# Second inverse norm of the output projection behind four output additions, and five sums of squares moved from GpSimd to VectorE, in a one-layer Fourier / RG-LRU / PEER kernel

## The chip, the cores and the metric

The kernel runs on one core of a Trainium2 chip. The time is device microseconds (us) of one launch; the lower the better. The engines are named as in the profile: PE is the matrix engine (PEld its weight loads), DVE is VectorE, ACT is ScalarE, POOL is GpSimd, SP is the engine that issues most transfers.

## The reference

One layer works on 512 latent tokens of width 1024, with 256 context tokens that feed the recurrences. What matters here is the middle, where two head groups are normalised, joined, projected and added, and the second norm is taken:

```python
rx = ((lat_dirs[0] + lat_dirs[1]) * gelu(gx)).astype(x.dtype)
mx = concatenate([rmsnorm(fourier_mix(fx), fourier_out_g[l]),
                  rmsnorm(rx, lru_out_g[l])], axis=-1) @ w_out[l]
x = x + g1_x * mx
h2x = modulate(rmsnorm(x, norm2_g[l]), sh2_x, sc2_x)
x = x + g2_x * peer_ffn(h2x, ...)
```

`rmsnorm` multiplies by the inverse root of the mean square over the width. `peer_ffn` makes queries from `h2x`, takes the best keys, and sums the experts that they choose out of a table of 16384; it is by far the longest part of the run.

## The kernel before

Everything is kept transposed: width on the 128 partitions (eight blocks `x2[0]` to `x2[7]` of 128x512), tokens along the row. Float32 products are made of three matmuls of a high and a low part (`mm3`), so each operand is split: ACT writes the high part (`act(hi, ...)`), DVE or POOL the low part, a subtraction.

The output projection is the loop `for k in range(8)` near the end of the first phase. `out_mm(k)` multiplies half of the normalised heads by one block of output weights into two PSUM banks: k = 0 to 3 use the Fourier heads `Ys`, k = 4 to 7 the recurrent heads `mr`. There are five such banks (tag "ps"), so `out_mm(0)`, `out_mm(1)` and the first half of `out_mm(2)` fill them, and the next half must wait until an `out_add` has read one.

- `out_add(k, ..., rF)` for k < 4 multiplies a bank by the gate and by the Fourier inverse norm `rF` on DVE (L650, reads PSUM and one SBUF tile) and adds the product to `x2` on POOL (L651, reads two SBUF tiles). For k of 4 and more one DVE instruction adds the bank to `x2` (L647).
- `rsqrt` (L148 to L154) makes an inverse norm: one ACT instruction, then L151 (DVE, reads PSUM) and L152, L153, L154 (DVE, each with two SBUF tiles), each needing the one before. It is called for `rF` and for `r`, the inverse norm of the recurrent branch.
- `rec_norm(k)` makes one of the four tiles of `mr`: `rx * r` on POOL (L630, two SBUF tiles), high part on ACT, low part on DVE (L579). `out_mm(4)` needs all four.
- `out_weights(k)` splits a block of output weights: high part `whi` on ACT, low part `wlo` on DVE (L123).
- `x2_sums(k)` squares two blocks of `x2` on ACT and adds the squares of blocks 0 to 5 up in `sq2` (L669); blocks 6 and 7 and `sq2` are then summed over the partitions by matmuls with ones (L666, L667, L664), which gives `rstd2`. Blocks 0 and 1 are squared after `out_add(5)`, 2 and 3 after `out_add(6)`, 4 and 5 after `out_add(7)`.

Behind the loop stand the last columns of the modulation (`mod_mm(20)` to `mod_mm(23)`, L232, and `half_turned(23)`, L240), then the second norm (L742, L744 and ACT), which makes `h2h` and `h2l`, on which all of `peer_ffn` rests. The splits of the first query weights (`wpq`, on DVE) and of the first expert weights `u` (on POOL, L123 as well) are already under way here.

PE, ACT and DVE run the first phase in the order in which the code is written: `in_order` ties each instruction to the one before on its engine. POOL's and SP's order is the scheduler's.

Of the kernel before, what the change touches and what calls it, by code (L numbers as in the profile page):

```python
# [9 lines left out]
F32 = mybir.dt.float32  # L10
# [5 lines left out]
ALU = mybir.AluOpType  # L16
# [35 lines left out]
def build(tc, xT, ctxT, c2t, vecs, wm, wu, wf, wg, wgate, wo, wq, keys, u, v, urow, vrow,  # L52
# [3 lines left out]
    V, S, G, PE = nc.vector, nc.scalar, nc.gpsimd, nc.tensor  # L56
# [8 lines left out]
    def act(o, i, f, bias=None, scale=None, **kw):  # L65
        if bias is not None:
            kw["bias"] = bias
        if scale is not None:
            kw["scale"] = scale
        return S.activation(o, i, f, **kw)  # L70
# [32 lines left out]
    def tact(*a, **kw):  # L103
        ins = act(*a, **kw).ins
        after(ins, last[0], "activation table order")
        last[0] = ins

    def pst(tag="ps", n=512, dt=F32):
        return psum.tile([P, n], dt, tag=tag, name="ps_" + tag, bufs={"ps": 5, "pm": 1, "pa": 2}[tag])

    def load(ap, st="", cuts=1):
        t = raws.tile([P, 2048], F32, tag="raw" + st, name="raw")
        n = 2048 // cuts
        for c in range(cuts):
            nc.sync.dma_start(t[:, c * n:(c + 1) * n], ap[:, c * n:(c + 1) * n])
        return t
# [9 lines left out]
    def split_w(raw, h, lo_eng=None, st=""):  # L126
        return split((wspl.tile([P, 1024], F32R, tag="whi" + st, name="whi"),
                      wspl.tile([P, 1024], F32R, tag="wlo" + st, name="wlo")),
                     raw[:, h * 1024:(h + 1) * 1024], lo_eng)
# [18 lines left out]
    def rsqrt(r, m, ss, n):  # L148

        tact(r, ss, AF.Abs_reciprocal_sqrt, bias=epst, scale=1.0 / n)  # L150
        V.tensor_scalar(m, ss, 1.0 / n, EPS, op0=ALU.mult, op1=ALU.add)  # L151
        V.scalar_tensor_tensor(m, m, -0.5, r, op0=ALU.mult, op1=ALU.mult)  # L152
        V.tensor_tensor(m, m, r, op=ALU.mult)  # L153
        V.scalar_tensor_tensor(r, m, 1.5, r, op0=ALU.add, op1=ALU.mult)  # L154
# [10 lines left out]
    def bt(dt=F32, n=L):  # L165
        return bp.tile([P, n], dt, tag="b", name="b")
# [18 lines left out]
    def mod_load_b(n):  # L185

        rawm[n] = ahead.get(n) or [bt()[:, :512] for j in range(4)]
        for j, t in enumerate(rawm[n]):
            nc.sync.dma_start(t, wm[n // 8, n % 8, :, j * 512:(j + 1) * 512])
# [29 lines left out]
    def mod_mm(n):  # L219
        t = rawm.pop(n)  # L220
        if n < 8 or n >= 16:


            m, first, final = -1 - n // 4, n % 4 == 0, n % 4 == 3
            ds = [2 * (n % 4) + j // 2 for j in range(4)]
        else:
            m, first, final = n // 8, n % 8 == 0, n % 8 == 7
            ds = [n % 8] * 4
        if first:
            modp[m] = pst("pm")  # L230
        for j in range(4):
            PE.matmul(modp[m][32 * j:32 * j + 32], cc32[:, ds[j]], t[j], start=first, stop=final)  # L232

    def half_turned(n):

        sb = bt(F32, 512)
        act(sb, modp[-1 - n // 4], AF.Copy)
        pT = pst("pa", 32)
        for b in range(4):
            PE.matmul(pT[:, 4 * b:4 * b + 4], sb[:, b * P:(b + 1) * P], vec[:, V_SEL2:V_SEL2 + 4], start=True, stop=True)  # L240
        return pT[:, :16].rearrange("p (b j z) -> p z j b", b=4, j=2)

    def half_biased(pv, o, outs):
        for k, mm in enumerate(outs):
            V.tensor_tensor(mm[:, o:o + 8].rearrange("p (j b) -> p j b", j=2), pv[:, k],
                            vec[:, V_BMOD + o:V_BMOD + o + 8].rearrange("p (j b) -> p j b", j=2), op=ALU.add)
# [220 lines left out]
    def mod_cols(w, st=""):  # L467
        mod_load(8 + w, st)
        if w:
            mod_mm(7 + w)  # L470
        if w == 8:
            mod_out(1)
# [67 lines left out]
    def out_weights(k):  # L540
        wp = split_w(rawo[k // 2], k % 2, V, ("", "U")[k // 2 % 2])
        if k % 2 and k < 4:
            rawo.append(load(wo[2 + k // 2]))
        return wp
# [83 lines left out]
    def rec_norm(k):  # L628
        rx = hsum[k][:, C:]
        G.tensor_tensor(rx, rx, r, op=ALU.mult)  # L630
        mr.append(scaled_split(rx, vec[:, V_LG + k:V_LG + k + 1]))

    def out_mm(k, wp, ms):
        pss = []
        for e in range(2):
            ps = pst("ps")
            for c in range(NB):
                o = (e * 4 + c) * P
                mm3(ps, cut(wp, slice(o, o + P)), ms[c], c == 0, c == NB - 1)
            pss.append(ps)  # L640
        return pss

    def out_add(k, pss, r=None):
        for e in range(2):
            d = 2 * (k % 4) + e
            if r is None:
                V.scalar_tensor_tensor(x2[d], pss[e], mods[:, 16 + d:17 + d], x2[d], op0=ALU.mult, op1=ALU.add)  # L647
            else:
                t = bt(F32, 512)
                V.scalar_tensor_tensor(t, pss[e], mods[:, 16 + d:17 + d], r, op0=ALU.mult, op1=ALU.mult)  # L650
                G.tensor_tensor(x2[d], x2[d], t, op=ALU.add)  # L651

    sq2 = bt(F32, 512)
    ss2 = []

    def x2_sums(k):
        if k == 3:
            ss2.append(pst("pa"))
        for e in range(2):
            d = 2 * k + e  # L660
            sq = bt(F32, 512) if d else sq2
            act(sq, x2[d], AF.Square)
            if d == ND - 1:
                PE.matmul(ss2[0], ones, sq, start=False, stop=True)  # L664
            elif d == ND - 2:
                PE.matmul(ss2[0], ones, sq2, start=True, stop=False)  # L666
                PE.matmul(ss2[0], ones, sq, start=False, stop=False)  # L667
            elif d:
                G.tensor_tensor(sq2, sq2, sq, op=ALU.add)  # L669

    psk = {}
    for k in range(8):
        psk[k] = out_mm(k, wpo[k], Ys if k < 4 else mr)
        if k == 1:
            ssf, ssr = pst("pa"), pst("pa")
            PE.matmul(ssf, ones, Y0, start=True, stop=True)
            PE.matmul(ssr, ones, sqr, start=True, stop=True)
            rF = bt(F32, 512)
            rsqrt(rF, bt(F32, 512), ssf, 512)
            r = bt(F32, 512)  # L680
            rsqrt(r, bt(F32, 512), ssr, 512)
            out_add(0, psk[0], rF)
        if k:
            out_add(k, psk[k], rF if k < 4 else None)
        if k > 4:
            x2_sums(k - 5)
        if k + 4 < 8:
            wpo[k + 4] = out_weights(k + 4)
        if 0 < k < 3:
            rec_norm(2 * k - 2)  # L690
            rec_norm(2 * k - 1)
        if k < 3:
            mod_cols(9 + k, "U")
        if k == 3:
            mod_mm(19)
        if k == 5:
            half_biased(half_turned(19), 32, (mods,))
        if k in (3, 4):
            mod_load_b(14 + 2 * k)
            mod_load_b(15 + 2 * k)  # L700
        if k == 5:
            raw0 = load(wq[0])
        if k == 6:
            wpq = [split_w(raw0, p, V) for p in range(2)]
    x2_sums(3)
    rsqrt(rstd2, bt(F32, 512), ss2[0], 1024)
    for n in range(20, 24):
# [257 lines left out]
    for ch in range(NCH):  # L965
# [14 lines left out]
        for q in range(TC // 4):  # L980
            ps = pst()
            for t in range(4):
                o = ps[:, t * P:(t + 1) * P]
                k, r = 2 * q + t // 2, t % 2
# [226 lines left out]
    for g in order:  # L1211
# [9 lines left out]
        sq = phase_v(g, cur, nxt)  # L1221
# [101 lines left out]
```

## Time and profile before

| | us |
|---|---|
| median of 3 runs | 1462.14 |
| lowest and highest of them | 1456.86, 1463.33 |
| the profiled execution | 1457.23 |
| its span, first to last instruction | 1455.5 |
| PE busy | 1386.5 |
| DVE busy | 1234.6 |
| POOL busy | 685.3 |

The output projection and the second norm lie between 185 and 250 us of the span. The times in the rows below are microseconds from the start of the span.

### The profile page before, as it was taken

The page shows a single profiled execution, that of the slowest core. Times are in us where ns is not written, and L with a number is a line of the kernel's source. Part 1 is how long each engine was busy: PE and PEld are TensorE (multiplying, and loading weights), DVE is VectorE, ACT ScalarE, POOL GpSimd, SP SyncE. Part 2 cuts the span into 40 slices and gives each one's busy share as a digit, 9 for nine tenths or more (in the row PEclk, how much of TensorE's full clock was granted, in tenths as well). Part 3 has the DMA queues.
Part 4 walks back from the last instruction along what each step waited for, and adds up shares of the span by engine and source line. Part 5 has one row for each costly group of instructions (what it writes and reads, how often), then busy time and mean ns, then how long its engine had stood idle before and what let it go on. Part 6 is the DMA issues. An engine that isn't in the chain of part 4 may idle for free. (4 is left out here: it accounts for less than half of the span.)

```text
span 1455.5 us, 22655 instructions
## 1 busy us (share of the span) xinstructions
PE 1386.5 (95%) x8577; PEld 1282.2 (88%) x8577; DVE 1234.6 (85%) x2185; ACT 614.5 (42%) x882; POOL 685.3 (47%) x462
## 2 busy tenths in 40 slices
PE   6998898999989999999999999999999999899995
PEld 2776766888969999999999999999999999899995
DVE  5677876599987999598998889999898989999973
ACT  4567634433434656434343432434333343243351
POOL 0044163666520000465666757675675766644412
PEclk9999999999999999999999999999999999999997
DMA  9334465331326999999999998999999999999901
GB/s 348 153 116 150 169 230 183 136 114 63 112 91 202 307 302 319 365 379 355 399 373 416 337 394 328 413 376 379 406 377 375 390 364 416 409 415 416 394 33 57
DMA packets 133645, 420.61 MB, mean 289 GB/s; under 512 B 10784, under 2 KB 60192, under 8 KB 110496
## 3 DMA queue, kind: packets, MB, share of 16 engines
q1 hardware_dynamic: 86976, 251.04, 46.5%
q0 software_dynamic: 46560, 168.14, 29.9%
q8 instruction: 67, 1.10, 0.3%
q14 instruction: 42, 0.34, 0.1%
HBM read 385.41 MB, written 33.69 MB: 288 GB/s over the span
## 5 line engine op out<-in xcount | busy, mean ns | idle before, releaser
L70 ACT ACTIVATE whi<-raw 128x1024 fp32r<-128x1024 f32 x296 | 312.7, 1060 | 589.1 <-PE ps_pa L133 291.6
L123 DVE TENSOR_TENSOR wlo<-raw,whi 128x1024 fp32r<-128x1024 f32 x264 | 327.0, 1241 | 41.4 <-ACT whi L70 39.3
L132 PE MATMUL ps_pa<-h2h,whi 128*128 128x352 f32 x1024 | 334.9, 327 | 3.2 <-ACT act L70 3.2
L134 PE MATMUL ps_pa<-h2h,wlo 128*128 128x352 f32 x1024 | 333.0, 325 | 0.2 <-DVE wlo L123 0.2
L133 PE MATMUL ps_pa<-h2l,whi 128*128 128x352 f32 x1024 | 332.6, 325 | 0.0
L1106 POOL DMA_INDIRECT row<-vrow,eidx x128 | 193.4, 1511 | 131.9 <-DVE oacc L1127 95.1
L1106 POOL DMA_INDIRECT row<-urow,eidx x128 | 198.3, 1549 | 110.7 <-DVE row L1113 56.8
L133 PE MATMUL ps_ps<-wl,whi 128*128 128x352 f32 x640 | 207.3, 324 | 0.0
L134 PE MATMUL ps_ps<-wh,wlo 128*128 128x352 f32 x640 | 206.7, 323 | 0.1
L132 PE MATMUL ps_ps<-wh,whi 128*128 128x352 f32 x640 | 206.1, 322 | 0.0
L132 PEld LDWEIGHTS ps_pa<-h2h,whi 128*128 128x128 f32 x1024 | 192.9, 188 | 5.3 <-ACT act L70 4.0
L134 PEld LDWEIGHTS ps_pa<-h2h,wlo 128*128 128x128 f32 x1024 | 192.7, 188 | 1.4 <-DVE wlo L123 0.5
L133 PEld LDWEIGHTS ps_pa<-h2l,whi 128*128 128x128 f32 x1024 | 192.7, 188 | 1.1
L1113 DVE SCALAR_TENSOR_TENSOR row<-row,hrow 128x1024 f32<-128x1024 f32 x128 | 153.6, 1218 | 32.6 <-DMA row<-urow,eidx 32.4
L1127 DVE SCALAR_TENSOR_TENSOR oacc<-row,gw,oacc 128x1024 f32<-128x1024 f32 x127 | 162.4, 1279 | 8.6 <-DMA row<-vrow,eidx 8.1
L134 PEld LDWEIGHTS ps_ps<-wh,wlo 128*128 128x128 f32 x640 | 120.2, 188 | 0.4 <-DVE wlo L123 0.4
L133 PEld LDWEIGHTS ps_ps<-wl,whi 128*128 128x128 f32 x640 | 120.2, 188 | 0.0
L132 PEld LDWEIGHTS ps_ps<-wh,whi 128*128 128x128 f32 x640 | 120.1, 188 | 0.0
L123 POOL TENSOR_TENSOR wlo<-raw,whi 128x1024 fp32r<-128x1024 f32 x32 | 77.5, 2422 | 84.1 <-ACT whi L70 57.8
L133 PE MATMUL ps_pa<-wl,whi 128*128 128x352 f32 x256 | 82.9, 324 | 0.0
L134 PE MATMUL ps_pa<-wh,wlo 128*128 128x352 f32 x256 | 82.6, 323 | 0.0
L132 PE MATMUL ps_pa<-wh,whi 128*128 128x352 f32 x256 | 82.3, 322 | 0.0
(303 smaller groups left out, 2606.4 us busy)
## 6 DMA issues: line engine op xcount, KB each, us to landing
raw<-u SPq DMA_DIRECT2D x64, 1024.0 KB
raw<-v SPq DMA_DIRECT2D x64, 1024.0 KB
Gd<-stg SPq DMA_DIRECT2D x22, 1024.0 KB
gt<-Gd SPq DMA_DIRECT2D x16, 1408.0 KB
raw<-wm SPq DMA_DIRECT2D x16, 1024.0 KB
b<-wm SPq DMA_DIRECT2D x32, 256.0 KB
raw<-wq SPq DMA_DIRECT2D x8, 1024.0 KB
Ad<-act SPq DMA_DIRECT2D x10, 704.0 KB
```

The costliest lines, as they stand in the source:

```text
L70: return S.activation(o, i, f, **kw)
L123: lo_ins[0] = (lo_eng or V).tensor_tensor(dst[1], src, dst[0].bitcast(F32), op=ALU.subtract).ins
L132: PE.matmul(ps, a[0], b[0], start=start, stop=False)
L133: PE.matmul(ps, a[0], b[1], start=False, stop=False)
L134: PE.matmul(ps, a[1], b[0], start=False, stop=stop)
L1106: G.indirect_dma_start(out=t, out_offset=None, in_=tab, in_offset=bass.IndirectOffsetOnAxis(ap=e[:, s:s + 1], axis=0))
L1113: ins = V.scalar_tensor_tensor(t, t, 1.0, hr, op0=ALU.mult, op1=ALU.mult, accum_out=dt[:, s:s + 1])
L1127: ins = V.scalar_tensor_tensor(o, t, g[:, s:s + 1], o, op0=ALU.mult, op1=ALU.add)
```

## The change

Two edits. The call that makes `r` now stands behind `out_add(0)` and `out_add(1)`. And the additions into `sq2` (five: blocks 1 to 5) go to VectorE instead of GpSimd.

```diff
             elif d:
-                G.tensor_tensor(sq2, sq2, sq, op=ALU.add)
+                V.tensor_tensor(sq2, sq2, sq, op=ALU.add)
...
             rF = bt(F32, 512)
             rsqrt(rF, bt(F32, 512), ssf, 512)
-            r = bt(F32, 512)
-            rsqrt(r, bt(F32, 512), ssr, 512)
             out_add(0, psk[0], rF)
         if k:
             out_add(k, psk[k], rF if k < 4 else None)
+        if k == 1:
+            r = bt(F32, 512)
+            rsqrt(r, bt(F32, 512), ssr, 512)
```

On DVE, at `k == 1` of the loop, the difference reads as follows (`-` is before, `+` is after; `ps_ps` are the banks of `out_mm`, `ps_pa` the sum of squares, `b` SBUF tiles of the first phase).

```order
 L154 SCALAR_TENSOR_TENSOR b<-b 128x512
+L650 SCALAR_TENSOR_TENSOR b<-ps_ps,mods,b 128x512 x4
 L151 TENSOR_SCALAR b<-ps_pa 128x512
 L152 SCALAR_TENSOR_TENSOR b<-b 128x512
 L153 TENSOR_TENSOR b<-b 128x512
 L154 SCALAR_TENSOR_TENSOR b<-b 128x512
-L650 SCALAR_TENSOR_TENSOR b<-ps_ps,mods,b 128x512 x4
 L123 TENSOR_TENSOR wlo<-raw,whi 128x1024
 L579 SCALAR_TENSOR_TENSOR b<-b,vec 128x512 x2
```

The four products of the first two output additions have moved ahead of the four instructions that make `r`; what follows stands as it did.

On POOL, at the same place, the scheduler answers with another order (`x_83` to `x_90` are `x2[0]` to `x2[7]`).

```order
 L588 TENSOR_TENSOR b<-b 128x512 x3
-L630 TENSOR_TENSOR b<-b 128x512 x2
 L651 TENSOR_TENSOR x_83<-x_83,b 128x512
-L630 TENSOR_TENSOR b<-b 128x512
 L651 TENSOR_TENSOR x_84<-x_84,b 128x512
-L630 TENSOR_TENSOR b<-b 128x512
 L651 TENSOR_TENSOR x_85<-x_85,b 128x512
 L651 TENSOR_TENSOR x_86<-x_86,b 128x512
+L630 TENSOR_TENSOR b<-b 128x512 x4
 L651 TENSOR_TENSOR x_87<-x_87,b 128x512
```

Before, two of the four products with `r` stood ahead of the first addition to `x2` and the other two between the next ones; now all four stand behind four such additions.

On DVE again, at the end of the loop, around the splits of the first query weights.

```order
 L647 SCALAR_TENSOR_TENSOR x_87<-ps_ps,mods,x_87 128x512
 L647 SCALAR_TENSOR_TENSOR x_88<-ps_ps,mods,x_88 128x512
+L669 TENSOR_TENSOR b<-b 128x512 x2
 L123 TENSOR_TENSOR wlo<-raw,whi 128x1024 x2
 L647 SCALAR_TENSOR_TENSOR x_89<-ps_ps,mods,x_89 128x512
 L647 SCALAR_TENSOR_TENSOR x_90<-ps_ps,mods,x_90 128x512
+L669 TENSOR_TENSOR b<-b 128x512 x2
 L151 TENSOR_SCALAR b<-ps_pa 128x512
```

Four of the five moved additions stand here, two ahead of the weight splits and two behind the last output addition; the fifth stands earlier, behind `x_86`. On SP one load of expert weights (`raw<-u`) moves ahead of the 16 loads `b<-wm` of the last modulation columns; PE's and ACT's orders are unchanged, and so is every order behind the second norm.

## Rows read from the trace of the kernel before

**Rows 1.** The page: busy time, share of the span and instructions of each engine.

```profile
PE 1386.5 (95%) x8577; PEld 1282.2 (88%) x8577; DVE 1234.6 (85%) x2185; ACT 614.5 (42%) x882; POOL 685.3 (47%) x462
```

**Rows 2.** Busy time by stretch: length; PE, PEld, DVE, ACT, POOL; clock, DMA, GB/s.

```profile
185.00:200.00 15.00, 12.68 (x58) 7.99 (x51) 8.45 (x12) 4.26 (x5) 4.63 (x3) 1.00 0.55 206
200.00:215.00 15.00, 14.79 (x70) 10.03 (x69) 15.00 (x14) 4.91 (x6) 15.00 (x10) 1.00 0.72 262
215.00:235.00 20.00, 18.93 (x87) 15.46 (x86) 11.49 (x12) 8.03 (x12) 14.24 (x9) 1.00 0.80 281
235.00:246.00 11.00, 7.78 (x49) 3.24 (x48) 5.55 (x11) 3.98 (x7) 2.97 (x2) 1.00 0.60 213
262.00:300.00 38.00, 38.00 (x206) 33.54 (x205) 29.51 (x172) 16.02 (x26) 26.42 (x19) 1.00 0.28 97
600.00:800.00 200.00, 200.00 (x1245) 200.00 (x1244) 178.86 (x217) 75.60 (x97) 124.00 (x82) 1.00 0.98 384
```

**Rows 3.** Timeline of PE: start, length, instruction, [idle before it <- what ended it].

```profile
199.44 0.50 PE L132 MATMUL ps_ps<-b,whi 128*128 128x512 f32 x1 [2.33 <-DVE b L650]
...
212.83 0.50 PE L133 MATMUL ps_ps<-b,whi 128*128 128x512 f32 x1 [0.21 <-DVE b L579]
...
234.67 1.12 PE L666 MATMUL ps_pa<-b,ones 128*128 128x512 f32 x2 [1.06 <-POOL b L669]
...
236.49 1.02 PE L664 MATMUL ps_pa<-b,ones 128*128 128x512 f32 x2
...
245.36 0.50 PE L132 MATMUL ps_ps<-h2h,whi 128*128 128x512 f32 x1 [2.36 <-ACT h2h L70]
```

**Rows 4.** Timeline of DVE in the first half of the output projection.

```profile
195.25 0.69 DVE L154 SCALAR_TENSOR_TENSOR b<-b 128x512 f32<-128x512 f32 x1
...
198.03 0.69 DVE L154 SCALAR_TENSOR_TENSOR b<-b 128x512 f32<-128x512 f32 x1
198.64 2.72 DVE L650 SCALAR_TENSOR_TENSOR b<-ps_ps,mods,b 128x512 f32<-128x512 f32 x4
201.28 1.21 DVE L123 TENSOR_TENSOR wlo<-raw,whi 128x1024 fp32r<-128x1024 f32 x1
202.41 1.77 DVE L579 SCALAR_TENSOR_TENSOR b<-b,vec 128x512 fp32r<-128x512 f32 x1
...
210.99 1.78 DVE L579 SCALAR_TENSOR_TENSOR b<-b,vec 128x512 fp32r<-128x512 f32 x1
```

**Rows 5.** Timeline of POOL and ACT at the same place.

```profile
198.80 2.53 POOL L630 TENSOR_TENSOR b<-b 128x512 f32<-128x512 f32 x2 [10.24 <-DVE b L154]
201.29 2.34 POOL L651 TENSOR_TENSOR x<-x,b 128x512 f32<-128x512 f32 x1
...
207.01 1.28 POOL L630 TENSOR_TENSOR b<-b 128x512 f32<-128x512 f32 x1
...
200.11 0.73 ACT L70 ACTIVATE b<-b,vec 128x512 fp32r<-128x512 f32 x1 [5.26 <-POOL b L630]
```

**Rows 6.** Timeline of DVE and POOL at the loop's end.

```profile
228.28 0.75 DVE L647 SCALAR_TENSOR_TENSOR x<-ps_ps,mods,x 128x512 f32<-128x512 f32 x1 [1.97 <-PE ps_ps L134]
...
230.08 3.41 DVE L123 TENSOR_TENSOR wlo<-raw,whi 128x1024 fp32r<-128x1024 f32 x1
...
233.41 1.40 DVE L647 SCALAR_TENSOR_TENSOR x<-ps_ps,mods,x 128x512 f32<-128x512 f32 x2
...
229.17 3.24 POOL L123 TENSOR_TENSOR wlo<-raw,whi 128x1024 fp32r<-128x1024 f32 x1 [0.76 <-ACT whi L70]
232.37 2.25 POOL L669 TENSOR_TENSOR b<-b 128x512 f32<-128x512 f32 x1
```

**Rows 7.** PE's clock around a wait late in the run: timeline, then busy time by stretch.

```profile
1243.05 0.66 PE L133 MATMUL ps_pm<-wl,whi 128*128 128x352 f32 x1 [4.99 <-DVE wl L123]
...
1238.00:1242.00 4.00, 0.06 (x1) 0.00 (x0) 3.96 (x4) 1.51 (x2) 1.98 (x2) 1.00 1.02 409
1242.00:1246.00 4.00, 2.95 (x10) 2.95 (x11) 4.00 (x6) 0.00 (x0) 2.37 (x2) 0.58 1.02 413
```

## The prediction

> **What bounds the kernel now.** I read the page first, then a table of stretches, then the timelines of PE, DVE and POOL from 185 to 250 us. PE is busy 95% of the span [rows 1]; behind the second norm it stays full for long stretches, 38 of 38 us and 200 of 200 [rows 2], and all of that work rests on `h2`. So whatever the second norm starts later or earlier, the end of the run does too; I carry every microsecond of it through. In the changed place PE loses time four times [rows 3]: 2.33 us at 199.44, because all five banks are full and the first L650 stands behind the making of `r`; 0.21 us at 212.83, waiting for the last low part of `mr` (L579); 1.06 us at 234.67, waiting for POOL's last addition L669; and 2.36 us ahead of `h2`. Between 200 and 215 us DVE and POOL are both busy 15.00 of 15.00 us [rows 2], and that is the point: PE's wait is 0.21 us there, but the chain `r`, L630, high part, L579 ends only at 212.77 us (210.99 + 1.78, rows 4), so it has no slack at all. Time won for PE at 199 is of use only if this chain also ends earlier.
>
> **How DVE and POOL share.** POOL's L630 pair (1.27 us each) and DVE's L650 (0.68 each, one operand in PSUM) run side by side at full pace from 198.64 on [rows 4, 5]. Not so where the DVE instruction has two SBUF tiles: L651 starts at 201.29 beside L123 (1.21 us) and takes 2.34 us, that is, it ends 1.2 us after L123 does; L579 starts at 202.41 and takes 1.77 us, ending 0.55 us after that L651 ended at 203.63 [rows 4, 5]. I read this as turns: one waits until the other's instruction is over, and they alternate. Free of it, a 128x512 addition costs 1.25 us on POOL [rows 5], a two-tile instruction of DVE 0.65 us (the 0.69 of L154 less its overlap with the next, rows 4).
>
> **Part 1, `r` behind four L650.** Nothing is removed, only moved. Times on the axis of the trace before:
> - L650 x4 start when the first L154 is nearly done, 195.86 instead of 198.64, and end at 198.58. The first bank is free at 196.6, so PE's 2.33 us go.
> - Their products release POOL: L651 runs 196.7 to 198.0, to 199.2, to 200.45. These stand ahead of L630 now.
> - DVE makes `r`: L151 at 198.5 reads PSUM and is not held. L152 is due at 199.23 and finds the third L651: it runs 200.45 to 201.05. The fourth L651 takes its turn to 202.3; L153 to 202.95, L154 to 203.6. So `r` is there at 203.6; before it was there at 198.72 (198.03 + 0.69): 4.9 us later, of which 2.7 are the four L650 and 2.2 the turns.
> - From here the turns go on. DVE's L123 to 204.7; L630 to 205.95; high part (0.73, rows 5) and L630 number two to 207.15; L579 to 207.8; L630 number three to 209.0; L579 to 209.65; L630 number four to 210.85; two L650 and L123 on DVE, one or two L651 on POOL, to 214.4; the last two L579 to 215.8. The chain ends at 215.8 instead of 212.77: +3.0 us. L579 now stands in DVE's queue waiting for POOL; behind it are `out_add(2)`, `out_add(3)` and the weight splits, and PE waits for their banks and tiles, but later than for `mr`.
> - PE reaches `out_mm(4)` 2.3 us earlier, at 207.7, works a little, then stands from about 210.4 to 215.2. From the resumption on it is 3.0 us late.
>
> The trace before shows no rsqrt of DVE beside a busy POOL. If its two-tile instructions were not held, `r` would be there at 201.4, and the same counting ends at 214.1: +1.35 us. With one more turn lost it is +4.3. I take +3.0, since L152 and L154 are the same operation as L579, which is held [rows 4]. The Trainium skill's page "SBUF — State Buffer", section "SBUF: two separate sides", says that a VectorE instruction with two SBUF inputs and a GpSimd one that reads SBUF lock each other out for the whole instruction; by that rule it is +3.0, without it +1.35.
>
> **The clock in that gap.** PE idle for 4.99 us at 1238 came back at half its clock: the stretch 1242 to 1246 has a granted clock of 0.58, where 1.00 is 2.4 GHz and 0.50 is 1.2 GHz [rows 7]. The gap of 2.33 us at 197 left it at 1.00 [rows 2]. The new gap of 4.7 us is like the former: of 2.95 busy us half is lost, 1.5 us. Bounds: 0 and 1.7.
>
> **Part 2, L669 on DVE.** An addition costs 0.65 instead of 1.25 us, but what counts is where it stands. Take times without the shift of part 1, which moves all of this alike. Before, the last one waits for POOL's L123 and ends at 234.62 [rows 6]; that sets L666 at 234.67 [rows 3]. Now, from 228.28: L647 to 228.95; L669 to 229.6; here POOL's L123 (229.17) takes its turn of 2.3 us to 231.9 (before, it ended at 232.41, 2.33 after the first DVE split made way at 230.08); L669 to 232.55; two L123 of 1.15 to 234.8 (the second took 3.41 before, for it was the one that waited); two L647, 1.35, to 236.15; two L669, the second needing the first, to 237.5. L666 follows at 237.5: +2.85 us against 234.67. L667, L664, the modulation columns, L240 and the norm stand behind it on PE in a fixed order, so all are +2.85; the block squares on ACT are there in time. If POOL's split met none of it, the sum would be 235.3, +0.6; if it took two turns of 2.3, +5.2. I take the one turn, as the trace has one now. The page "Perfetto Trace Analysis", section "Optimizing GPSIMD Operations", of the Trainium skill says to prefer other engines to GPSIMD where possible; by that rule the 1.06 us in front of L666 would go, and only the place in DVE's queue, behind two splits and two output additions, speaks against it.
>
> **SP** issues one load of `u` ahead of the 16 `b<-wm`; it waits for PE's reading of a modulation block that is over by 207.7. I cost it at nothing: these columns are wanted only behind L664, at 237 us or later, and the transfers before took some 13 us from 204.
>
> **Sum.** 3.0 + 1.5 + 2.85 = +7.35 us. On the profiled execution that is 1457.2 to 1464.6. That execution lies 4.9 us under the median, near the lowest of the runs; I add the same to the median: 1462.1 + 7.35 = 1469.5, and call it 1469. About 0.5%, that is 7.3 us, is what a measurement of this kernel can tell from no change, so the forecast sits on that edge.
>
> **Rivals.**
> - Lighter: rsqrt is not held by POOL, the clock does not fall, POOL's split slips past. +1.35 + 0.6 to +1.35 + 2.85, so 1464 to 1466.5. For it: no row shows the first two. Against: [rows 4, 5, 7]. It is within 0.5%.
> - Faster: the chain through `r` decides nothing and the sums arrive sooner. The 2.33, 0.21 and 1.06 us go: 1458.5. It decides at `out_mm(4)`: it holds only if the last L579 ends before 210.4. Against: that needs the fully busy DVE and POOL of [rows 2] to save 2.4 us while `r` comes later. By the Trainium skill's preference for other engines (the page and section named in part 2) that part alone would give 1461, with the same small chance.
> - Heavier: in part 2 PE stands 3.9 us ahead of L666, and then works lightly; a second stretch at 1.2 GHz costs up to 1.7 us, one more turn on DVE 1.3 to 2.3: +10 to +11.5, 1472 to 1473.5. For it: 235 to 246 is thin already, 7.78 of 11 us [rows 2].
>
> **How the numbers follow.** Forecast 0.55, lighter 0.2, heavier 0.2, faster 0.05. The forecast's own spread (turns, clock, and runs that differ by 6 us) puts half of it above 7.3 us. Slower by over 0.5%: 0.27 + 0.2 = 0.47. Same: 0.28 + 0.2 + 0.02 = 0.5. Faster: 0.03, since even that rival is only -0.25%. The range leaves out the faster case and the ends of the spread: 1462 to 1475; the forecast alone is 1467 to 1472.
>
> **What would show it.** L650 at about 195.9 and no wait of PE at 197; then a wait of 4 to 5 us ended by L579 inside `out_mm(4)`, and a granted clock under 1.00 behind it; the L152 or L153 of `r` longer than 1.2 us; POOL's L630 starting near 204.7; L666 waiting for DVE's L669 for 3 to 4 us instead of POOL's for 1.06; `h2` starting near 252 to 253 instead of 245.4; everything behind it unchanged. I am wrong in part 1 if the last L579 ends before 214, in part 2 if L666 waits under 2 us, and in the carrying through if `h2` is late but the end is not.

## The result

| | before | after |
|---|---|---|
| median, us (7 runs each) | 1462.22 | 1471.81 |
| lowest and highest | 1456.86, 1463.33 | 1470.39, 1474.26 |
| profiled execution | 1457.23 | 1470.39 |
| its span | 1455.5 | 1468.6 |

The medians lie 9.6 us apart. The changed kernel takes 1.0071 times as long, 95% interval [1.0051, 1.0090]: 0.7% slower, 7.5 to 13.2 us, and the whole interval lies above the 0.5% that the prediction named. The forecast of 1469 was 2.8 us short, and the case that came true, slower by over 0.5%, had the second largest chance, 0.47.

The starts and the ends of these runs differ by some microseconds without an edit (last section). So from here on I compare the part that the change touches by its own length: from the first matmul that sums the squares of the Fourier branch over the partitions (L676; L677 does the same for the recurrent branch) to the first matmul with `h2h`. I call it **the stage**. Before, it runs from 191.30 to 245.36, 54.06 us; after, from 194.76 to 257.79, 63.03 us, that is +8.97. Behind it the run takes 1210.1 us before (1455.5 - 245.36) and 1210.8 after, so in this pair the loss is not behind the stage.

The stage starts 3.46 us later in after's trace (194.76 - 191.30); that has to be taken off a time of after to set it beside one of before. The engines' totals hardly tell (page, busy time and share; compare [rows 1]):

```profile
PE 1394.3 (95%) x8577; PEld 1287.5 (88%) x8577; DVE 1237.6 (84%) x2190; ACT 614.7 (42%) x882; POOL 679.3 (46%) x457
```

PE executes the same 8577 matmuls and is busy 7.8 us longer: a matmul that runs at the lower clock counts as busy time. The timeline of PE says where (start, length, instruction, idle time before it and what ended it; the rows answer to [rows 3]):

```profile
194.76 1.02 PE L676 MATMUL ps_pa<-b,ones 128*128 128x512 f32 x2
...
212.91 0.51 PE L133 MATMUL ps_ps<-b,whi 128*128 128x512 f32 x1 [0.75 <-DVE b L579]
...
218.03 0.79 PE L133 MATMUL ps_ps<-b,whi 128*128 128x512 f32 x1 [4.16 <-DVE b L579]
...
245.54 1.12 PE L666 MATMUL ps_pa<-b,ones 128*128 128x512 f32 x2 [3.86 <-DVE b L669]
...
248.01 1.91 PE L664 MATMUL ps_pa<-b,ones 128*128 128x512 f32 x2
...
257.79 0.77 PE L132 MATMUL ps_ps<-h2h,whi 128*128 128x512 f32 x1 [2.28 <-ACT h2h L70]
```

The wait of 2.33 us for L650 is gone. In its place stand 4.16 us inside `out_mm(4)`, and the wait ahead of L666 has grown from 1.06 to 3.86 us. A pair of matmuls with ones, 1.02 us before (L664, [rows 3]), takes 1.91. By stretch (columns of [rows 2]; the first row has the limits of a row there, but the stage begins 3.46 us later in it):

```profile
185.00:200.00 15.00, 15.00 (x69) 9.85 (x69) 7.35 (x8) 7.07 (x9) 5.44 (x3) 1.00 0.44 160
213.00:218.00 5.00, 0.88 (x3) 0.39 (x3) 5.00 (x5) 1.73 (x3) 4.43 (x3) 0.80 0.90 307
218.00:222.70 4.70, 4.67 (x11) 3.70 (x12) 4.41 (x5) 0.26 (x1) 3.32 (x2) 0.50 1.05 400
246.70:250.00 3.30, 3.30 (x8) 0.82 (x10) 0.00 (x0) 0.05 (x1) 0.99 (x1) 0.50 0.81 243
```

PE is full up to 200 now, 15.00 of 15.00 us. Behind each of the two long waits it works at a granted clock of 0.50, 1.2 GHz, for 4.70 us and for 3.30 us.

On DVE and POOL the turns are there to be read. Timeline of DVE, to be set beside [rows 4]:

```profile
199.44 0.75 DVE L650 SCALAR_TENSOR_TENSOR b<-ps_ps,mods,b 128x512 f32<-128x512 f32 x1
...
202.09 0.68 DVE L151 TENSOR_SCALAR b<-ps_pa 128x512 f32<-128x512 f32 x1
202.80 1.83 DVE L152 SCALAR_TENSOR_TENSOR b<-b 128x512 f32<-128x512 f32 x1
204.66 1.67 DVE L153 TENSOR_TENSOR b<-b 128x512 f32<-128x512 f32 x1
206.37 0.69 DVE L154 SCALAR_TENSOR_TENSOR b<-b 128x512 f32<-128x512 f32 x1
206.97 1.22 DVE L123 TENSOR_TENSOR wlo<-raw,whi 128x1024 fp32r<-128x1024 f32 x1
...
217.90 0.74 DVE L579 SCALAR_TENSOR_TENSOR b<-b,vec 128x512 fp32r<-128x512 f32 x1
```

and of POOL, beside [rows 5]:

```profile
200.28 1.30 POOL L651 TENSOR_TENSOR x<-x,b 128x512 f32<-128x512 f32 x1 [8.24 <-DVE b L650]
...
204.02 1.76 POOL L651 TENSOR_TENSOR x<-x,b 128x512 f32<-128x512 f32 x1
...
207.13 2.21 POOL L630 TENSOR_TENSOR b<-b 128x512 f32<-128x512 f32 x1 [1.35 <-DVE b L154]
```

L152 and L153 of `r`, which have two SBUF tiles, take 1.83 and 1.67 us while POOL's additions L651 are queued; L151, which reads PSUM, takes its usual 0.68 beside the same additions, and L154, for which POOL has nothing left, 0.69. POOL's fourth L651 is held in turn, 1.76 us instead of 1.3. `r` is there at 207.06 (206.37 + 0.69).

### The profile page after: what moved, and what is told of

Read it like the earlier page. It is cut to its first block, busy times and chain, and to the rows that moved or that the text cites. A ratio compares the mean times of both kernels' runs of the same rounds, so it can differ in the third digit from the quotient of the medians.

```text
span 1468.6 us, 22646 instructions
## 1 busy us (share of the span) xinstructions
PE 1394.3 (95%) x8577; PEld 1287.5 (88%) x8577; DVE 1237.6 (84%) x2190; ACT 614.7 (42%) x882; POOL 679.3 (46%) x457
## 5 line engine op out<-in xcount | busy, mean ns | idle before, releaser
L123 DVE TENSOR_TENSOR wlo<-raw,whi 128x1024 fp32r<-128x1024 f32 x264 | 325.1, 1234 | 42.8 <-ACT whi L70 40.8
L123 POOL TENSOR_TENSOR wlo<-raw,whi 128x1024 fp32r<-128x1024 f32 x32 | 77.2, 2413 | 103.1 <-ACT whi L70 76.8
```

The source lines that it names most:

```text
L123: lo_ins[0] = (lo_eng or V).tensor_tensor(dst[1], src, dst[0].bitcast(F32), op=ALU.subtract).ins
```

## The experiments

Each run was profiled, and timed against the kernel before on the same chip. Ratios are to the kernel before of the same runs; its own medians were 1462.22 to 1466.08 us from one set of runs to the next, so medians of different rows are not to be compared. "to L666" and "stage" are counted from the start of L676 in the profile, "rest" from `h2h` to the end of the span. Where an edit adds lines, the same instructions have higher line numbers (L678 to L683 for L676, L668 to L673 for L666); the text keeps the old ones.

| kernel | to L666 | stage | rest | ratio, 95% interval | median, us |
|---|---|---|---|---|---|
| before | 43.37 | 54.06 | 1210.1 | | |
| before_again | 43.37 | 54.05 | 1212.5 | 0.9988 [0.9966, 1.0010] | 1462.99 |
| after | 50.78 | 63.03 | 1210.8 | 1.0071 [1.0051, 1.0090] | 1471.81 |
| after_again | 50.57 | 62.87 | 1214.8 | 1.0063 [1.0024, 1.0102] | 1472.69 |
| r_moved_only | 47.95 | 58.64 | 1213.6 | 1.0022 [1.0005, 1.0038] | 1467.82 |
| sums_moved_only | 46.13 | 59.28 | 1214.4 | 1.0036 [1.0016, 1.0055] | 1467.89 |
| products_first | 49.52 | 62.66 | 1211.5 | 1.0063 [1.0039, 1.0087] | 1473.87 |
| busy_gaps | 48.71 | 59.28 | 1217.5 | 1.0058 [1.0033, 1.0082] | 1471.73 |
| additions_held | 44.43 | 56.73 | 1213.8 | 1.0016 [0.9993, 1.0039] | 1466.13 |
| sums_earlier | 42.10 | 53.22 | 1213.5 | 0.9996 [0.9978, 1.0013] | 1462.44 |
| chain_first | 40.30 | 51.43 | 1216.3 | 0.9969 [0.9950, 0.9988] | 1459.52 |

The theory: part 1 costs by the turns between POOL's additions and DVE's making of `r`, part 2 by its place in DVE's queue, and behind the wait that each leaves, PE comes back at half its clock. The rivals: one part does all the harm, or the loss comes out of something else (transfers, the order behind the norm).

**The unchanged kernels once more.**

> The kernel before, unchanged, profiled once more: the stage from L676 to the first h2h should be 54.06 us again within 0.3. It tells how much the stretch ahead of L676 (191.30 us in the first profile, 191.0 to 194.8 in the others) and the stretch behind the first h2h (1210.1 us, 1210.8 to 1217.5 in the others) change from execution to execution with no edit at all. My theory: both move by 1 to 5 us by themselves. Rival: they are fixed by the kernel, 191.3 and 1210.1 again, and the edits reach further than the stage.

> The kernel with both edits, unchanged, profiled once more: the stage should be 63.03 us again, or up to 1.7 off where the clock falls at another moment. L676 was at 194.76 us and the rest 1210.8 us. My theory: L676 anywhere from 191 to 195 us, the rest anywhere from 1210 to 1218. Rival: 194.8 and 1210.8 again.

The stage comes back within 0.16 us in both (54.05, 62.87). The rest does not: 2.4 us more in the one, 4.0 in the other. The stage is the measure for this change, and a difference of a few us in a profile's total says nothing.

**r_moved_only:** part 1 alone; the sums are back on POOL (against the kernel after).

```diff
-                V.tensor_tensor(sq2, sq2, sq, op=ALU.add)
+                G.tensor_tensor(sq2, sq2, sq, op=ALU.add)
```

> Only the making of r is moved behind the four L650; the sums of squares stay on POOL. I measure the stage from the first matmul of L676 to the first matmul with h2h: 54.06 us before (191.30 to 245.36), 63.03 us with both edits (194.76 to 257.79). My theory: PE's 2.33 us at out_mm(2) go, r comes some 5 us later because POOL's four L651 take turns with L152 and L153, PE waits 4 to 5 us in out_mm(4) and works at half clock behind it: +4.6 us, a stage of 58 to 59 us, the time 0.3% above before. Rival: the move gives back the 2.33 us and everything lost comes from the other edit: a stage of 51.6 us.

The stage is 4.58 us longer than before, and all of it is there at L666 already (47.95 - 43.37 = 4.58). PE's timeline shows the wait of after in `out_mm(4)`, and the short one of before ahead of L666:

```profile
216.63 0.80 PE L133 MATMUL ps_ps<-b,whi 128*128 128x512 f32 x1 [4.15 <-DVE b L579]
...
241.35 1.12 PE L666 MATMUL ps_pa<-b,ones 128*128 128x512 f32 x2 [1.07 <-POOL b L669]
```

So part 1 is a loss by itself: the end of PE's wait at 199 was paid back with more.

**sums_moved_only:** part 2 alone (against the kernel before).

```diff
-                G.tensor_tensor(sq2, sq2, sq, op=ALU.add)
+                V.tensor_tensor(sq2, sq2, sq, op=ALU.add)
```

> Only the five additions of the sums of squares go to VectorE; r is made where it was. My theory: the last two of them wait in VectorE's queue behind two weight splits and two output additions, and the splits behind a POOL split: L666 waits 3.9 us instead of 1.06, and the light work behind it runs partly at half clock: +2.8 to +4 us, a stage (L676 to the first h2h) of 57 to 58 us. Rival, by the cheaper addition (0.69 us against 1.29 to 2.25): L666 starts at the end of out_mm(7), -1.06 us, a stage of 53.0 us.

PE's timeline has the old wait at 200 and the new one ahead of L666; the stretch behind it stands under it (columns of [rows 2]):

```profile
200.28 0.50 PE L132 MATMUL ps_ps<-b,whi 128*128 128x512 f32 x1 [2.33 <-DVE b L650]
...
238.26 2.07 PE L666 MATMUL ps_pa<-b,ones 128*128 128x512 f32 x2 [3.86 <-DVE b L669]
```

```profile
238.20:243.40 5.20, 5.14 (x6) 1.85 (x6) 0.01 (x1) 0.09 (x1) 2.21 (x1) 0.50 0.83 321
```

L666 is 2.76 us later (46.13 - 43.37), and 2.46 more are lost between it and `h2h`, where PE works at 0.50; here even L666 itself is at that clock, 2.07 us for the pair instead of 1.12. I had expected a stage of 57 to 58; it is 59.28, for 2.46 us are lost behind L666, where I had allowed up to 1.2. The parts alone make 4.58 + 5.22 = 9.80 us, together 8.97: they add up but for 0.8. No single part does the harm.

**products_first:** the kernel after, but POOL makes the four products with `r` (L630) ahead of the additions to `x2` (L651). It tests whether the order on POOL is to blame for part 1.

```diff
...
-                G.tensor_tensor(x2[d], x2[d], t, op=ALU.add)
+                adds.append(lambda d=d, t=t: G.tensor_tensor(x2[d], x2[d], t, op=ALU.add).ins)
...
+        if k in (2, 3):
+            prev = recs[-1]
+            while adds:
+                ins = adds.pop(0)()
+                after(ins, prev, "additions behind the products with r")
+                prev = ins
```

> Both edits, but POOL is told to run its four products with r (L630 of the kernel before) ahead of all additions to x2 (L651). r is still made behind the four L650. My theory, that it is POOL's order and its turns with r that cost: r at +2.7 us instead of +4.9, no addition between the products, the last L579 1.5 us earlier than in the kernel before; PE keeps the 2.33 us that it won up to 0.8 us, no half clock in out_mm(4): stage 56 to 57 us, of which +3 to +4 are the sums. Rival, that the lateness of r itself decides (four L650 in front, 2.7 us): the last L579 2.7 us late, stage 60 to 61 us.

My expectation failed. I had counted on 56 to 57; the stage is 62.66, only 0.4 better than after. The timeline of DVE, then of POOL (the additions are L653 here), then of PE, and the two stretches around PE's wait:

```profile
208.24 2.25 DVE L123 TENSOR_TENSOR wlo<-raw,whi 128x1024 fp32r<-128x1024 f32 x1
210.41 3.42 DVE L579 SCALAR_TENSOR_TENSOR b<-b,vec 128x512 fp32r<-128x512 f32 x2
```

```profile
209.37 2.24 POOL L653 TENSOR_TENSOR x<-x,b 128x512 f32<-128x512 f32 x1
211.57 1.72 POOL L653 TENSOR_TENSOR x<-x,b 128x512 f32<-128x512 f32 x1
```

```profile
212.21 0.79 PE L133 MATMUL ps_ps<-b,whi 128*128 128x512 f32 x1 [3.14 <-DVE b L579]
```

```profile
209.00:212.20 3.20, 0.07 (x1) 0.00 (x0) 3.20 (x3) 0.86 (x1) 3.20 (x3) 0.90 0.87 306
212.20:218.20 6.00, 5.96 (x13) 4.27 (x14) 5.75 (x5) 0.15 (x1) 6.00 (x4) 0.50 0.98 330
```

The additions did not go away: they stood behind the products and took turns with DVE's L123 (2.25 instead of 1.2 us) and with the last two L579 (3.42 for the pair; one takes 0.74 undisturbed, as the last in after). The last L579 ends 22.80 us from L676, 1.1 earlier than in after (218.64 - 194.76 = 23.88) and still 1.3 later than before (212.77 - 191.30 = 21.47). The wait that is left, 3.14 us, has the stretch at 0.50 behind it, which takes most of the gain back. So the theory of the order on POOL is too narrow. `r` itself is not held here: with no addition running yet, L152 and L153 take 0.69 us each. The mended theory is that any POOL instruction on SBUF costs that runs while the chain from `r` to the last L579 is on DVE; additions_held tests it.

**busy_gaps:** the kernel after, with 12 more matmuls in each of PE's two waits. Nothing reads their bank. It puts a price on the clock alone.

```diff
             for c in range(NB):
                 o = (e * 4 + c) * P
+                if k == 4 and e == 0 and c == 2:
+                    idle = pst("pa")
+                    for n in range(12):
+                        PE.matmul(idle, wp[0][:, :P], ms[0][0], start=n == 0, stop=n == 11)
...
             elif d == ND - 2:
+                idle = pst("pa")
+                for n in range(12):
+                    PE.matmul(idle, mr[1][0][:, :P], mr[0][0], start=n == 0, stop=n == 11)
                 PE.matmul(ss2[0], ones, sq2, start=True, stop=False)
```

> Both edits, and 12 matmuls of no use (128x512, about 0.23 us each, into a bank that nothing reads) in each of PE's two new waits: ahead of the third tile of mr in out_mm(4), and ahead of L666. My theory, that the idle time also takes the clock down: the granted clock stays at 1.00 in both places, 2.4 us are won in out_mm(4) and 1 to 1.7 us behind L666: stage 59 to 60 us instead of 63.03. Rival, that the clock falls for another reason or costs nothing: 63 us or more, by what the added matmuls cost.

PE's timeline, and the stretches behind the two waits:

```profile
212.06 2.91 PE L642 MATMUL ps_pa<-b,whi 128*128 128x512 f32 x12
...
216.65 0.50 PE L133 MATMUL ps_ps<-b,whi 128*128 128x512 f32 x1 [1.45 <-DVE b L579]
```

```profile
216.60:221.30 4.70, 4.65 (x20) 3.81 (x21) 4.70 (x6) 0.23 (x1) 3.30 (x2) 1.00 1.05 399
242.00:245.00 3.00, 2.93 (x10) 1.22 (x14) 0.00 (x0) 0.14 (x2) 2.13 (x1) 1.00 0.77 306
```

Of the same 4.70 us behind the same L579, PE makes 20 matmuls here and 11 in after. The stage is 59.28, so the clock is worth 3.75 us of after's 63.03: 2.07 up to L666 (50.78 - 48.71) and 1.68 behind it (12.25 - 10.57). The total cannot tell: its interval [1.0033, 1.0082] holds the 1.0071 of after as well as the 1.0045 that 3.75 us less would make. That the clock costs 3.75 us in the stage is shown; a gain for the whole run is not.

**additions_held:** products_first, and the additions wait for the last low part of `mr`. It tests the mended theory: with only the products with `r` left on POOL beside the chain, the turns with the additions go.

```diff
                 after(ins, prev, "additions behind the products with r")
+                if prev is recs[3]:
+                    tc.add_manual_dep(ins, low[0].name, mybir.DependencyInfo(...Sync...), reason="additions held")
                 prev = ins
```

> As products_first, and in addition POOL's eight additions to x2 must wait for the last low part of mr (the fourth L579 of the kernel before). In products_first the products with r came first, but the queued additions then held the weight split and the last two L579 on VectorE: 22.8 us from L676 to the end of the last L579, 21.5 before, and PE's wait of 3.14 us brought the half clock. My theory, mended: it is any POOL work beside the chain. Held back, the last L579 ends 19.7 us behind L676, PE waits 2 us or less in out_mm(4), the clock stays at 1.00 there, L666 comes at 44 to 45 us (before 43.4, products_first 49.5) and the stage to the first h2h is 56 to 57.5 us, all of the loss being the sums. Rival, that r being made 2.7 us later is enough: the wait stays over 3 us and the stage over 60 us.

DVE, POOL and PE (L581 is L579 here, L655 the addition):

```profile
200.62 0.69 DVE L152 SCALAR_TENSOR_TENSOR b<-b 128x512 f32<-128x512 f32 x1
201.35 0.69 DVE L153 TENSOR_TENSOR b<-b 128x512 f32<-128x512 f32 x1
...
209.80 1.21 DVE L123 TENSOR_TENSOR wlo<-raw,whi 128x1024 fp32r<-128x1024 f32 x1
...
211.59 0.74 DVE L581 SCALAR_TENSOR_TENSOR b<-b,vec 128x512 fp32r<-128x512 f32 x1
```

```profile
212.41 1.29 POOL L655 TENSOR_TENSOR x<-x,b 128x512 f32<-128x512 f32 x1 [2.71 <-DVE b L581]
```

```profile
211.73 0.50 PE L133 MATMUL ps_ps<-b,whi 128*128 128x512 f32 x1 [1.09 <-DVE b L581]
```

```profile
211.70:217.00 5.30, 5.27 (x23) 4.34 (x24) 4.50 (x6) 0.80 (x2) 4.58 (x3) 1.00 0.91 320
```

L152 and L153 of `r`, in the same place as in after, take 0.69 us each instead of 1.83 and 1.67; the L123 ahead of the last two L581 is back at 1.21 us, the last L581 at 0.74. The last low part ends 19.75 us from L676 (19.7 was expected), 4.1 earlier than in after and 1.7 earlier than before; PE's wait is 1.09 us and the clock stays at 1.00. The stage is 56.73, as expected. What is left over before is part 2: the chain is 1.72 us earlier, the sums cost their 2.76 as in sums_moved_only, and L666 comes 1.06 later (44.43 - 43.37); the other 1.61 us of the stage lie behind L666, which waits 3.86 us here as in after and has half the clock behind it (after loses 1.56 there).

**sums_earlier:** part 2 alone, with the additions written where their inputs are ready: ahead of the next output addition, and ahead of the splits of the first query weights.

```diff
-        if k:
-            out_add(k, psk[k], rF if k < 4 else None)
         if k > 4:
             x2_sums(k - 5)
+        if k:
+            out_add(k, psk[k], rF if k < 4 else None)
...
-        if k == 6:
-            wpq = [split_w(raw0, p, V) for p in range(2)]
     x2_sums(3)
+    wpq = [split_w(raw0, p, V) for p in range(2)]
```

> r as before the change. The five additions on VectorE, but written ahead of the output addition that follows their squares, and the two splits of the first query weights behind the last output addition. My theory, that the place in VectorE's queue costs and not the engine: L666 starts when out_mm(7) ends, 42.3 us behind L676 (before 43.4, sums_moved_only 46.1), the stage is 52.5 to 53.5 us (54.06 and 59.28). Rival, that VectorE is too full for these additions anyhow: L666 not before 45 us, the stage 57 us or more.

DVE's timeline: the last L669 is over at 233.45 (the first row is one of a pair), ahead of the last two L647, and PE has no wait ahead of L666 (L647 on DVE, then L666 on PE):

```profile
230.75 2.70 DVE L669 TENSOR_TENSOR b<-b 128x512 f32<-128x512 f32 x1
233.37 0.74 DVE L647 SCALAR_TENSOR_TENSOR x<-ps_ps,mods,x 128x512 f32<-128x512 f32 x1
```

```profile
234.47 1.02 PE L666 MATMUL ps_pa<-b,ones 128*128 128x512 f32 x2
```

The stage is 53.22: 6.06 us better than with the same additions in the other place (59.28), and 0.84 better than before. L666 comes 1.27 us earlier than before (42.10 against 43.37), but 0.43 of that is lost behind it (11.12 against 10.69): the weight splits now stand ahead of the L151 of `rstd2`, which starts only as they end, at 240.31. The total can't tell it from before. The Trainium skill, page "Perfetto Trace Analysis", section "Optimizing GPSIMD Operations", says to prefer other engines to GPSIMD where possible. Here the engine alone was not what decided: on VectorE the same five additions lost 5.22 us in one place of its queue and won 0.84 in another, with the weight splits moved behind them. Moving the splits and leaving the additions on GpSimd was not run; it might have won as much, since before's wait ahead of L666 was for a GpSimd addition that stood behind a split of GpSimd held to 3.24 us [rows 6].

**chain_first:** sums_earlier, and part 1 in a smaller step: `out_add(0)` alone goes ahead of `r`, the products with `r` go ahead of the weight split, and the additions are held as above.

```diff
-            rsqrt(r, bt(F32, 512), ssr, 512)
             out_add(0, psk[0], rF)
+            rsqrt(r, bt(F32, 512), ssr, 512)
...
+        if k == 1:
+            for n in range(NB):
+                rec_norm(n)
         if k + 4 < 8:
             wpo[k + 4] = out_weights(k + 4)
-        if 0 < k < 3:
-            rec_norm(2 * k - 2)
-            rec_norm(2 * k - 1)
```

> The first two L650 ahead of r, then r, the other two L650, and at once all four tiles of mr, ahead of the weight splits and of out_add(2); POOL's additions to x2 held behind the last L579; the sums as in sums_earlier. My theory: PE waits neither at out_mm(2) (2.33 us before) nor in out_mm(4), L666 comes at 39.5 to 40.5 us behind L676 (before 43.4), the stage is 50 to 51 us (before 54.06) and the time 0.2 to 0.3% below before. Rival: a wait of another engine takes the place, the stage is 53 us or more and the time as before.

DVE (L654 is the product of the output addition), then PE (L670 is L666):

```profile
199.87 0.68 DVE L151 TENSOR_SCALAR b<-ps_pa 128x512 f32<-128x512 f32 x1
200.58 0.69 DVE L152 SCALAR_TENSOR_TENSOR b<-b 128x512 f32<-128x512 f32 x1
201.31 0.69 DVE L153 TENSOR_TENSOR b<-b 128x512 f32<-128x512 f32 x1
```

```profile
213.46 0.50 PE L132 MATMUL ps_ps<-b,whi 128*128 128x512 f32 x1 [0.38 <-DVE b L654]
...
234.16 1.02 PE L670 MATMUL ps_pa<-b,ones 128*128 128x512 f32 x2
```

With no addition queued on POOL, L152 and L153 of `r` are at 0.69 us again, behind two products instead of four. PE's waits of 2.33, 4.16 and 3.86 us are gone; one of 0.38 is left. The stage is 51.43 us, 2.63 under before (50 to 51 was expected, so it is 0.4 over). The median is 1459.52, ratio 0.9969 [0.9950, 0.9988]: faster than before by 0.3%, with 12 runs against 29 and an interval that lies below 1 by 0.12%; the 2.63 us of the stage would make 0.2%. It was not run beside after; against the common kernel before, the two intervals lie far apart.

## Why the prediction was right in its steps and short in its size

The working gave +7.35 us; the stage shows +8.97. Step by step, with after's times counted from L676 and before's from its own:

| step | predicted | measured |
|---|---|---|
| `r` is there | +4.9 | +4.88 (12.30 against 7.42) |
| last L579 ends | +3.0 | +2.41 (23.88 against 21.47) |
| half clock behind the wait | +1.5 | +2.20 |
| both, at `x2[5]`'s L647 | +4.5 | +4.61 (41.59 against 36.98) |
| part 2, at L666 | +2.85 | +2.80 (7.41 - 4.61) |
| L666 to `h2h` | 0 | +1.56 (12.25 against 10.69) |
| sum | +7.35 | +8.97 |

**The turns.** The sign that the prediction asked for, an L152 or L153 over 1.2 us, is there twice (1.83, 1.67), and `r` is as late as counted: 2.7 us for four L650 and 2.2 for the turns. That it is POOL's additions that hold DVE, and not the place, is shown by additions_held and products_first, where the same two instructions stand behind four L650 as in after, no addition runs beside them, and they take 0.69. The Trainium skill, page "SBUF — State Buffer", section "SBUF: two separate sides", says that a VectorE instruction with two SBUF inputs and a GpSimd one that reads SBUF shut each other out for the whole instruction. The trace agrees: L152 and L153 are held, L151, which reads PSUM, is not (0.68). Further down I gave DVE and POOL 0.6 us too many: 3.0 against 2.41.

**The clock behind `out_mm(4)`.** The mechanism was right, the size was off: 1.5 against 2.20. I took 2.95 busy us from [rows 7] for the whole stretch at half rate. Here it is 4.67 us at 0.50 (218.0 to 222.7), which loses 2.3. In that row of before the wait ended 3 us before the clock rose; how long the stretch is behind a wait differs, and my upper bound of 1.7 was too low. The 2.20 is a difference of two rows of the table; busy_gaps, which takes this stretch away, reaches L666 2.07 us earlier. That both steps together come out at 4.61 against 4.5 is luck: 0.59 too many for the turns and 0.70 too few for the clock cancel.

**Part 2.** The wait ahead of L666 is 3.86 us, in the 3 to 4 that I named, and sums_moved_only alone gives +2.76. The POOL split took its one turn: DVE's timeline of after has one of the two L669 at `x2[5]` stretched to 2.70 us,

```profile
237.02 0.68 DVE L669 TENSOR_TENSOR b<-b 128x512 f32<-128x512 f32 x1
237.81 2.70 DVE L669 TENSOR_TENSOR b<-b 128x512 f32<-128x512 f32 x1
...
244.79 0.69 DVE L669 TENSOR_TENSOR b<-b 128x512 f32<-128x512 f32 x1
```

and the last one ends 9.13 us after the start of the L647 ahead of them (245.48 - 236.35), where my count had 9.22. Those two splits and two output additions that stand between are the price: sums_earlier takes them away, and L666 comes 4.03 us earlier (42.10 against 46.13).

**The step that failed** is the one behind L666, "so all are +2.85": it carried the delay on to `h2` at no further price. The second stretch at half clock, which the prediction held for a rival up to 1.7 us, costs 1.56 there (2.46 in sums_moved_only). So `h2h` comes at 254.33 on the axis of before (257.79 - 3.46), behind the 252 to 253 that I had named as a sign. So of the heavier rival one half came true, the clock, and the other did not: DVE lost no further turn. busy_gaps shows both stretches at once: with PE kept at work in its waits, 3.75 us of the stage go, and the two rows of the table say 2.20 + 1.56 = 3.76 (by place 2.07 and 1.68).

**The carrying through** was not contradicted: the rest is 1210.8 us against 1210.1, and 1214.8 against 1212.5 in the second pair. Such a rest differs by more than that between two executions of one kernel, so the close match of the first pair is luck; but the loss by the timed runs, 7.5 to 13.2 us, holds the 8.97 of the stage. SP's moved load cost nothing that can be seen: the modulation columns did not wait for it in any profile.

**The sum against the bound.** With +7.35 the forecast sat on the 0.5% edge, and I gave "same" 0.50 and "slower" 0.47. The 1.6 us of clock that I left out decide that. I had listed a price for the second stretch and a row for it (7.78 of 11 us busy, [rows 2]) and still left it to a rival with a chance of 0.2. A wait ahead of L666 of 3.9 us was my own number, and the trace had one row for a wait of that kind, 4.99 us with half clock behind [rows 7], and one of 2.33 without [rows 3]; the longer was the nearer for 4.7, and for 3.9 neither was far. A third stood in the changed place itself and I did not read it: the clock of before is at 0.50 behind the wait of 2.36 us ahead of `h2h` (last section). The price belonged into the sum.

## What to carry to other kernels

When an instruction is moved up to end a short wait, follow what it releases: here four products on VectorE started four additions on GpSimd, and these held the chain that ended last anyway. Work moved to a faster engine lost here in one place of that engine's queue and won in another, where its inputs were ready and the weight splits no longer stood ahead; look for the place before the engine. And a wait that grows has a second price behind it, the matmuls that run at half the clock: put it into the sum wherever the same trace has a wait like it with half the clock behind.

## What the runs showed of the hardware

**Waits and the clock.** In the stage, waits of PE of 1.09 us (additions_held) and 2.33 us (before, sums_moved_only) left the granted clock behind them at 1.00. Waits of 3.14 (products_first), 3.86 (after, sums_moved_only, additions_held) and 4.16 us (after) had a stretch at 0.50 behind or already at their end, in which a matmul takes twice its time. I had not expected the one of 3.14. These are eight places in five kernels, not a rule, and the length of the wait alone does not decide. At the end of the stage PE waits 2.28 to 2.70 us for `h2h` in all eleven profiles, after thin work (7.78 of 11 us in before, [rows 2]), and every one of them has a stretch at 0.50 there. In before it is this one (columns of [rows 2]):

```profile
246.00:249.40 3.40, 3.40 (x10) 2.51 (x9) 3.40 (x6) 1.57 (x3) 0.00 (x0) 0.50 0.00 0
```

In before and in after its lost time counts in the rest.

**The rest of the run varies with the same clock.** No edit is made in the code ahead of L676 or behind the norm, and still L676 starts between 191.03 and 194.76 us, and the rest takes 1210.1 to 1217.5. The records of the granted clock, added up over all stretches at 0.50 from `h2h` to the end of the span, are 35.3 us in before (rest 1210.1), 36.6 in after (1210.8), 44.9 in chain_first (1216.3) and 46.7 in busy_gaps (1217.5). A line through all eleven profiles rises 0.50 us for each microsecond at 0.50, which is what half rate makes (correlation 0.86). Why one execution meets more of them than another is open. Ahead of L676 two rows show it, the first of before, the second of after, for the same part of the kernel (columns of [rows 2]):

```profile
40.00:55.00 15.00, 13.82 (x78) 11.77 (x79) 11.77 (x21) 10.12 (x18) 0.00 (x0) 1.00 0.54 210
```

```profile
40.00:55.00 15.00, 13.17 (x64) 10.50 (x62) 12.08 (x21) 10.71 (x19) 0.00 (x0) 0.89 0.54 226
```

In after the clock is 0.89 there and PE gets 14 matmuls less done. Added up ahead of L676, before has 6.8 us at 0.50 and after 13.7, which at half rate makes 3.4 us; but before_again has 13.7 as well and starts its stage at 192.47, so the clock is not all of it. The 13.1 us between the two profiled spans are 3.5 of such a start, 8.97 of the stage and 0.7 of the rest; the first of the three is not the change's, for products_first, which has both edits too, starts its stage at 191.03.
